# Attention blocks spread evenly over the token groups of queries, keys and values; W_o's first two weights split on GpSimd

## The chip, the cores and the metric

The kernel runs on one core of one Trainium2 chip. Its engines are TensorE (PE; PEld is its weight load), VectorE (DVE), ScalarE (ACT), GpSimd (POOL) and SyncE (SP, which here only issues loads and stores). The metric is the device time of one execution in microseconds. Of the kernel before there are three timed runs, 1322.33, 1322.56 and 1325.32 us; their median is 1322.56 us. A profile is taken of another execution.

## The reference, cut to what matters

Two decoder layers over 512 tokens of 1024 features in float32. The first mixes with a convolution module, the second with causal differential attention over 8 heads; each is followed by a SwiGLU FFN and by a gated per-layer input embedding. The change lies in the second layer's attention:

```python
def diff_attention(x, w_qkv, q_g, k_g, lq1, lk1, lq2, lk2, sub_g, w_o, rel_bias, lambda_init):
    qkv = x @ w_qkv
    q, k, v = jnp.split(qkv, 3, axis=-1)
    q = rms_norm(q.reshape(B, S, N_HEADS, 2, HEAD_DIM), q_g) * (HEAD_DIM ** -0.5)
    k = rms_norm(k.reshape(B, S, N_HEADS, 2, HEAD_DIM), k_g)
    v = v.reshape(B, S, N_HEADS, V_DIM)
...
        logits = jnp.einsum('bhcqd,bhckd->bhcqk', q_blk, k).astype(jnp.float32)
        logits = logits + bias[None, :, None]
        logits = jnp.where(dist >= 0, logits, -jnp.inf)
        probs = jax.nn.softmax(logits, axis=-1)
        w = probs[:, :, 0] - lam * probs[:, :, 1]
        return jnp.einsum('bhqk,bhkd->bhqd', w.astype(v.dtype), v)
...
    o = rms_norm(o, sub_g) * (1.0 - lambda_init)
    return o.reshape(B, S, N_HEADS * V_DIM) @ w_o
```

After it comes `h = h + swiglu(...)`, then `h = h + gate * (p[i] @ ple_w_proj[i])`. The product `p[i] @ ple_w_proj[i]` depends on no result of the layer, and the kernel computes it just behind the attention's slabs ("the projections" below).

## The kernel before, in words

**Products in three passes.** Every float32 product is computed with operands split into a high and a low part, as three matmuls (L142 to L144: low x high, high x low, high x high). A weight of 128x1024 is loaded by SP into a raw buffer (`wraw`, L133), ACT casts it to `whi` (L136), and DVE or POOL subtracts to get `wlo` (L137). There are 2 raw buffers and 4 each of `whi` and `wlo`. A load waits until the split of the weight that was in its raw buffer is done; a cast waits until PE is done with the weight that was in its `whi` buffer. The projections' input features pass through the same raw buffers (`pfeatures`, L238 load, L239 cast on ACT, L240 subtract on DVE).

**The slabs.** Queries with keys, and values, are computed in six slabs in the order of `QKV` (L69): q0, v0, q1, q2, v1, q3. A q slab holds queries and keys of a pair of heads, a v slab the values of four heads. A slab has four weights (`slab`, L556; from the second slab on its first weight is split on POOL, `GLO = 1`). It runs over four token groups of 128 tokens; each group is 24 matmuls of 512 columns into one PSUM tile (`tokens`, L564). A group of a q slab is a *unit*: ACT reads it twice (L600 scaled, L603 squared), DVE sums the squares (L607) and prepares them (L199), POOL raises to the power -1/2 (L201) and multiplies (L610), and then in `unit_end` PE transposes (L616), ACT writes queries and keys (L624, L625), POOL copies the keys' high part to the other half (L629), and DVE makes the remainders (L632, L634).

**The attention stages.** Every head has four blocks of 128 queries, and every block has three stages, 96 in all, in one list ordered so that a block's stages lie a few places apart: `stage_s` (PE scores L661, L662; DVE adds bias and takes the maximum L664; ACT exp L668; DVE combines L671 to L673), `stage_t` (PE transposes L681; ACT L683 and DVE L684 split), `stage_a` (PE with the values L697, L698; ACT L704, DVE L705; after a head's last block a norm, L709 to L719, POOL with L201 and L719). `stage_o` then transposes a finished head (L726) and splits it (`split_scaled`, L156 on ACT, L157 on DVE) into W_o's input. In the loop over the slabs the third item of a `QKV` entry gives for each token group how many steps of three stages are issued between its matmuls. The last `unit_end` follows the loop. What is left of the list is issued one stage at a time through `step()`: in the projections (L772 to L785, two weights, called P0 and P1 here, eight groups of six matmuls, L142 to L144 on `C` tiles), and then in W_o.

**W_o.** `linear` (L426) computes W_o's eight groups; the first two share a pass over the heads (`group0=2`), so their weights, called O0 and O1 here, are needed together. `first` says how many of these are split on POOL.

**What sets the order.** The program is handed to a scheduler that arranges each engine's instructions by its own model of their times; on the chip each engine then runs its list in order. An instruction that waits keeps all behind it on its engine waiting. PE's tiles come from 4 accumulators (`mm`), 2 score tiles (`sc`) and 2 transpose tiles (`tp`).

Of the kernel before, what the change touches and what calls it, by code (L numbers as in the profile page):

```python
# [23 lines left out]
NC = D // P  # L24
# [41 lines left out]
PACK = True  # L66
E1 = True
GLO = 1
QKV = (("q", 0, (0, 0, 0, 0)), ("v", 0, (0, 1, 1, 0)), ("q", 1, (1, 1, 2, 2)), ("q", 2, (0, 1, 2, 0)), ("v", 1, (1, 2, 2, 2)), ("q", 3, (0, 2, 0, 1)))  # L69


@with_exitstack
def trunk(ctx, tc, xT, pT, wts, diag, dww, vec, rel, onehot, lamv, out):
# [51 lines left out]
    def weight(n=1024, pieces=1, between=(), eng=V):  # L125
        i = wnext[0]
        wnext[0] += 1
        raw = sb([P, 1024], "wraw", 2)
        hi = sb([P, 1024], "whi", 4, F32R)
        lo = sb([P, 1024], "wlo", 4, F32R)  # L130
        for k in range(pieces):
            cut = slice(k * n // pieces, (k + 1) * n // pieces)
            nc.sync.dma_start(raw[:, cut], wts[i, :, cut])  # L133
            if k < len(between):
                between[k]()
            A.copy(hi[:, cut], raw[:, cut])  # L136
            eng.tensor_tensor(lo[:, cut], raw[:, cut], f(hi[:, cut]), ALU.subtract)  # L137
        return hi, lo

    def mm3(acc, a, b, first, last):  # L140
        (ah, al), (bh, bl) = a, b
        T.matmul(acc, al, bh, start=first, stop=False)  # L142
        T.matmul(acc, ah, bl, start=False, stop=False)  # L143
        return T.matmul(acc, ah, bh, start=False, stop=last)  # L144

    def wpart(w, k):
        return tuple(t[:, k * P : (k + 1) * P] for t in w)
# [254 lines left out]
    for m in range(NC):  # L402
        if m % 4 == 0:
            w = weight()
# [21 lines left out]
    def linear(n_in, src, consume, group0=1, before=None, after=None, first=0):  # L426


        m = 0
        while m < NC:  # L430
            g = group0 if m == 0 else 1
            ws = [weight(n_in * P, eng=G if m == 0 and i >= g - first else V) for i in range(g)]
            accs = [mm() for _ in range(g)]
            for k in range(n_in):
                if before:
                    before(k)
                for w_, a_ in zip(ws, accs):
                    mm3(a_, wpart(w_, k), src[k], k == 0, k == n_in - 1)
                    if after:
                        after()  # L440
            for i in range(g):
                consume(m + i, accs[i])
            m += g
# [112 lines left out]
    def slab(n=0):  # L556
        ws = [weight(eng=G if i < n else V) for i in range(4)]
        return [
            tuple(t[:, j * S : (j + 1) * S] for t in ws[k])
            for k in range(4)  # L560
            for j in range(2)
        ]
# [158 lines left out]
    ot = {}  # L721
# [22 lines left out]
    waiting = None  # L744
    for what, at, pace in QKV:
        ws = slab(GLO if at > 0 else 0)
# [27 lines left out]
    for m in range(NC):  # L774
        if m % 4 == 0:
            w = weight()
# [17 lines left out]
        V.tensor_tensor(h[m], acc, h[m], ALU.add)  # L794
        norm.chunk(m)

    linear(NC, ot, add_attn, 2, heads_until, step)
    n2 = Norm("ple_g1")
    ffn(norm, n2)

# [32 lines left out]
def _layout(a):  # L833
# [25 lines left out]
    qkv = a["attn_w_qkv"][0]  # L859
    for what, at, _ in QKV:  # L860
        if what == "v":
# [59 lines left out]
```

## Time and profile before

| | |
|---|---|
| median of three runs | 1322.56 us |
| the profiled execution | 1323.92 us |
| its span, first to last instruction | 1322.1 us |
| granted TensorE clock, mean | 0.986 of full |
| DMA | 91 GB/s mean |

The page gives for each engine the time in which it was busy. A row of a timeline has the start in us from the span's start, the duration, engine, line, operation, what is written and read with its shape, how many alike follow each other, and in brackets how long the engine stood idle before it and what it then waited for. Matmuls are pipelined: a row of 0.39 us is followed by the next 0.23 us later. A row of groups has the count, the total busy time, the mean of one in ns, and the idle time before with what ended it. A row of a table by stretches has the length and then each engine's busy time with its number of instructions, the granted clock, DMA's share and rate.

### The profile page before, as it was taken

The page shows a single profiled execution, that of the slowest core. Times are in us where ns is not written, and L with a number is a line of the kernel's source. Part 1 is how long each engine was busy: PE and PEld are TensorE (multiplying, and loading weights), DVE is VectorE, ACT ScalarE, POOL GpSimd, SP SyncE. Part 2 cuts the span into 40 slices and gives each one's busy share as a digit, 9 for nine tenths or more (in the row PEclk, how much of TensorE's full clock was granted, in tenths as well). Part 3 has the DMA queues.
Part 4 walks back from the last instruction along what each step waited for, and adds up shares of the span by engine and source line. Part 5 has one row for each costly group of instructions (what it writes and reads, how often), then busy time and mean ns, then how long its engine had stood idle before and what let it go on. Part 6 is the DMA issues. An engine that isn't in the chain of part 4 may idle for free. (4 is left out here: it accounts for less than half of the span.)

```text
span 1322.1 us, 15025 instructions
## 1 busy us (share of the span) xinstructions
PE 1284.4 (97%) x5686; PEld 1035.8 (78%) x5686; DVE 777.5 (59%) x1203; ACT 548.0 (41%) x862; POOL 303.8 (23%) x241
## 2 busy tenths in 40 slices
PE   8999879999999999999999998899999999999998
PEld 5766458888888888888888887778888888888887
DVE  6999984644344434455668897946543344334445
ACT  5676453422122212244466676734322222222342
POOL 5789852100000000022254544222000000000030
PEclk8999789999999999999999999999999999999999
DMA  6221112222222222222212221303222222222231
GB/s 222 90 104 52 51 32 86 90 96 96 100 96 99 100 100 96 80 101 101 91 64 81 103 73 36 108 34 126 97 96 96 96 98 100 103 94 93 78 121 64
DMA packets 37332, 120.40 MB, mean 91 GB/s; under 512 B 4323, under 2 KB 5475, under 8 KB 37260
## 3 DMA queue, kind: packets, MB, share of 16 engines
q1 hardware_dynamic: 35712, 117.06, 25.3%
q10 hardware_dynamic: 1548, 2.39, 0.6%
q8 instruction: 44, 0.72, 0.2%
q14 instruction: 28, 0.23, 0.0%
HBM read 117.31 MB, written 2.12 MB: 90 GB/s over the span
## 5 line engine op out<-in xcount | busy, mean ns | idle before, releaser
L136 ACT CAST whi<-wraw 128x1024 fp32r<-128x1024 f32 (+2 forms) x214 | 218.6, 1026 | 561.4 <-PE mm L144 351.3
L142 PE MATMUL mm<-A,wlo 128*128 128x512 f32 (+1 forms) x1096 | 426.8, 394 | 10.7 <-POOL C L597 6.0
L143 PE MATMUL mm<-A,whi 128*128 128x512 f32 (+1 forms) x1096 | 430.4, 394 | 0.2
L144 PE MATMUL mm<-A,whi 128*128 128x512 f32 (+1 forms) x1096 | 428.5, 391 | 0.0
L137 DVE TENSOR_TENSOR wlo<-wraw,whi 128x1024 fp32r<-128x1024 f32 (+2 forms) x207 | 259.1, 1255 | 62.4 <-ACT whi L136 62.3
L142 PEld LDWEIGHTS mm<-A,wlo 128*128 128x128 f32 x1096 | 208.2, 190 | 57.4 <-POOL C L597 6.8
L176 POOL TENSOR_TENSOR acc<-acc,wk 128x512 f32<-128x512 f32 x42 | 68.2, 1624 | 784.8 <-issue 671.2
L143 PEld LDWEIGHTS mm<-A,whi 128*128 128x128 f32 x1096 | 207.7, 190 | 47.4 <-DVE A L157 3.1
L144 PEld LDWEIGHTS mm<-A,whi 128*128 128x128 f32 x1096 | 207.8, 190 | 44.1 <-issue 1.9
L144 PE MATMUL mm<-B,whi 128*128 128x512 f32 x352 | 137.0, 389 | 0.0
L143 PE MATMUL mm<-B,whi 128*128 128x512 f32 x352 | 137.0, 389 | 0.0
L142 PE MATMUL mm<-B,wlo 128*128 128x512 f32 x352 | 136.4, 389 | 0.0
L305 POOL TENSOR_TENSOR wk<-wk,C 128x512 f32<-128x512 f32 x76 | 112.1, 1480 | 25.6 <-ACT C L304 19.6
L472 DVE TENSOR_TENSOR big<-mm,rb 128x512 f32<-128x512 f32 x44 | 30.4, 691 | 125.9 <-PE mm L144 125.9
L480 DVE TENSOR_TENSOR h<-mm,h 128x512 f32<-128x512 f32 x48 | 33.0, 691 | 120.9 <-PE mm L144 120.9
L470 DVE TENSOR_TENSOR big<-mm,rb 128x512 f32<-128x512 f32 x44 | 30.4, 691 | 99.3 <-PE mm L144 92.9
L143 PEld LDWEIGHTS mm<-B,whi 128*128 128x128 f32 x352 | 66.1, 188 | 13.7
L142 PEld LDWEIGHTS mm<-B,wlo 128*128 128x128 f32 x352 | 66.1, 188 | 13.7
L144 PEld LDWEIGHTS mm<-B,whi 128*128 128x128 f32 x352 | 66.1, 188 | 13.6
L144 PE MATMUL mm<-whi,A 128*128 128x512 f32 x192 | 75.7, 395 | 0.0
L143 PE MATMUL mm<-wlo,A 128*128 128x512 f32 x192 | 75.0, 396 | 0.0
L142 PE MATMUL mm<-whi,A 128*128 128x512 f32 x192 | 74.8, 397 | 0.0
(185 smaller groups left out, 1433.3 us busy)
## 6 DMA issues: line engine op xcount, KB each, us to landing
wraw<-in_wts SPq DMA_DIRECT2D x194, 512.0 KB, 3.4
wraw<-in_wts SPq DMA_DIRECT2D x16, 384.0 KB, 3.0
h<-in_xT SPq DMA_DIRECT2D x8, 256.0 KB, 5.7
bias<-scr ACTq DMA_DIRECT2D x8, 256.0 KB, 3.3
D<-in_diag SPq DMA_DIRECT2D x7, 256.0 KB, 3.9
out_t<-h SPq DMA_DIRECT2D x7, 256.0 KB, 2.0
wraw<-in_wts SPq DMA_DIRECT2D x4, 256.0 KB, 5.5
wraw<-in_pT SPq DMA_DIRECT2D x4, 256.0 KB, 2.9
```

The costliest lines, as they stand in the source:

```text
L136: A.copy(hi[:, cut], raw[:, cut])
L137: eng.tensor_tensor(lo[:, cut], raw[:, cut], f(hi[:, cut]), ALU.subtract)
L142: T.matmul(acc, al, bh, start=first, stop=False)
L143: T.matmul(acc, ah, bl, start=False, stop=False)
L144: return T.matmul(acc, ah, bh, start=False, stop=last)
L176: self.eng.tensor_tensor(self.acc, self.acc, sq, ALU.add)
L305: G.tensor_tensor(pacc, pacc, pr, ALU.add)
L470: V.tensor_tensor(tg, pg, rb, ALU.mult)
L472: V.tensor_tensor(tu, pu, rb, ALU.mult)
L480: V.tensor_tensor(h[m], acc, h[m], ALU.add)
```

## The change

```diff
-QKV = (("q", 0, (0, 0, 0, 0)), ("v", 0, (0, 1, 1, 0)), ("q", 1, (1, 1, 2, 2)), ("q", 2, (0, 1, 2, 0)), ("v", 1, (1, 2, 2, 2)), ("q", 3, (0, 2, 0, 1)))
+
+QKV = tuple((w, i, (n,) * 4) for w, i, n in (("q", 0, 0), ("v", 0, 1), ("q", 1, 1), ("q", 2, 1), ("v", 1, 2), ("q", 3, 1)))
...
-    linear(NC, ot, add_attn, 2, heads_until, step)
+    linear(NC, ot, add_attn, 2, heads_until, step, first=2)
```

The first edit gives every token group of a slab the same number of steps: none in q0, one in v0, q1, q2 and q3, two in v1. Before it was a number for each group. The second edit makes POOL, not DVE, split O0 and O1. The set of instructions is otherwise the same; the scheduler arranges all engines anew from the second slab to W_o. The changed file has one line more, so a line number behind L69 is one higher there.

## The prediction

> **What bounds the kernel now.** I read the page first, then the sums by stretches around the end of the query/key/value stage, then PE's timeline there.
>
> ```profile
> span 1322.1 us, 15025 instructions
> ...
> PE 1284.4 (97%) x5686; PEld 1035.8 (78%) x5686; DVE 777.5 (59%) x1203; ACT 548.0 (41%) x862; POOL 303.8 (23%) x241
> ```
>
> PE is busy for 97% of the span, so only what fills or opens a hole on PE can matter. The change touches one stage, and there the picture differs:
>
> ```profile
> core 0: us, PE busy (x) PEld busy (x) DVE busy (x) ACT busy (x) POOL busy (x), PEclk, DMA share, GB/s
> 653.50:818.00 164.50, 162.32 (x841) 137.22 (x841) 126.33 (x327) 106.56 (x240) 78.58 (x75) 1.00 0.22 73
> 818.00:830.80 12.80, 6.51 (x34) 5.20 (x32) 12.17 (x33) 9.76 (x23) 4.78 (x6) 0.79 0.30 102
> 830.80:844.30 13.50, 10.95 (x57) 8.22 (x56) 13.36 (x34) 11.08 (x26) 3.88 (x4) 0.95 0.46 158
> 844.30:884.20 39.90, 38.93 (x221) 33.58 (x219) 24.43 (x74) 19.98 (x48) 6.14 (x6) 1.00 0.08 27
> ```
>
> The first stretch is the six slabs of queries, keys and values: PE misses 2.2 us of 164.5. In the next two PE misses 8.8 us while DVE misses 0.8: the tail of the attention is bound by DVE and the chains through it. After 844.3 PE is full again.
>
> ```profile
> 817.64 0.39 PE L144 MATMUL mm<-whi,A 128*128 128x512 f32 x1
> ...
> 828.44 0.66 PE L661 MATMUL sc<-C,C 128*128 128x384 f32 x1 [2.55 <-DVE st L672]
> ...
> 829.22 1.05 PE L616 MATMUL tp<-ident,big 128*128 128x128 f32 x4
> ...
> 830.80 0.80 PE L142 MATMUL mm<-C,wlo 128*128 128x512 f32 x1
> ...
> 832.20 0.39 PE L142 MATMUL mm<-C,wlo 128*128 128x512 f32 x1
> 832.42 0.39 PE L143 MATMUL mm<-C,whi 128*128 128x512 f32 x1
> ...
> 841.27 0.47 PE L661 MATMUL sc<-C,C 128*128 128x512 f32 x1
> ...
> 844.29 0.39 PE L142 MATMUL mm<-C,wlo 128*128 128x512 f32 x1
> ...
> 856.58 0.39 PE L142 MATMUL mm<-A,wlo 128*128 128x512 f32 x1
> ...
> 884.21 1.19 PE L142 MATMUL mm<-A,wlo 128*128 128x512 f32 x4 [0.78 <-ACT A L156]
> ```
>
> I put a clock's zero at the end of the last slab matmul: 817.64 plus one spacing (832.20 to 832.42, so 0.23 per 512 columns), 817.87. Then the first projection matmul stands at +12.9, the last unit's transposes at +11.3, the last unit's scores (head 6, block 3) at +23.4, unbroken projections from +26.4, the first W_o matmul at +38.7, the last W_o block at +66.3.
>
> **The change, part by part.** The pace tuples add up to 21 steps before and 24 after, so 72 of 96 attention stages instead of 63 are issued inside the slabs, and 24 instead of 33 afterwards. No instruction is added; two wlo splits go from DVE to POOL. The rest is order, and the built program lists it for each engine. These rows price it:
>
> ```profile
> L137 DVE TENSOR_TENSOR wlo<-wraw,whi 128x1024 fp32r<-128x1024 f32 x6 | 8.1, 1347 | 0.3 <-ACT whi L136 0.3
> L136 ACT CAST whi<-wraw 128x1024 fp32r<-128x1024 f32 x6 | 6.3, 1049 | 3.7 <-DMA wraw<-in_wts 3.7
> L157 DVE SCALAR_TENSOR_TENSOR A<-tp,lam,A 128x512 fp32r<-128x512 f32 x8 | 5.9, 746 | 5.0 <-ACT A L156 4.9
> L719 POOL TENSOR_TENSOR D<-D,r 128x512 f32<-128x512 f32 x4 | 5.1, 1269 | 4.0 <-DVE r L717 2.9 <-ACT D L704 1.1
> L201 POOL TENSOR_TENSOR r<-v,mhalf 128x4 f32<-128x4 f32 x4 | 4.0, 1007 | 35.4 <-DVE v L199 35.3
> L634 DVE SCALAR_TENSOR_TENSOR C<-tp,vec,C 64x256 fp32r<-64x256 f32 x7 | 3.4, 484 | 0.1
> L629 POOL CAST C<-C 64x256 fp32r<-64x256 f32 x6 | 2.9, 488 | 10.4 <-ACT C L625 10.4
> L624 ACT ACTIVATE C<-tp,lam 64x256 fp32r<-64x256 f32 x5 | 2.3, 468 | 0.5 <-PE tp L616 0.4
> L664 DVE CUSTOM_DVE_ANT_0 big<-sc,bias 128x512 f32<-128x512 f32 x3 | 2.1, 684 | 0.0
> L600 ACT ACTIVATE big<-mm,rcol 128x512 f32<-128x512 f32 x1 | 0.7, 688 | 0.0
> L607 DVE TENSOR_REDUCE v<-wk 128x8 f32<-128x512 f32 x1 | 0.7, 686 | 0.0
> ...
> wraw<-in_wts SPq DMA_DIRECT2D x194, 512.0 KB, 3.4
> ```
>
> *Slabs.* Over the two built orders, matmul by matmul at 0.23 us per 512 columns, 2.7 us of PE work moves ahead of the zero: **+2.7** there, given back in the tail below. DVE has 23% of the stretch free; the even pace asks for six stages in each group of the second value slab, three in the other groups and none in the first slab, so nothing bunches as in the old q1 and q3, but DVE has nine more stages to do. New waits: 0 if the slack takes them, 3 if they double today's 2.2; I take **+1.0**, nearer to the slack.
>
> *Projection weights come sooner.* P0 and P1 (line 776) share the raw buffers with the feature loads, so P0's load waits for L240.
>
> ```profile
> 823.21 0.68 DVE L240 TENSOR_TENSOR C<-wraw,C 128x512 fp32r<-128x512 f32 x1
> ...
> 829.52 1.23 DVE L137 TENSOR_TENSOR wlo<-wraw,whi 128x1024 fp32r<-128x1024 f32 x1 [0.31 <-ACT whi L136]
> ...
> 837.02 1.97 DVE L137 TENSOR_TENSOR wlo<-wraw,whi 128x1024 fp32r<-128x1024 f32 x1
> ...
> 828.44 1.05 ACT L136 CAST whi<-wraw 128x1024 fp32r<-128x1024 f32 x1 [2.60 <-DMA wraw<-in_wts]
> ```
>
> L240 ends at 823.89, +6.0, today; the load starts and its cast, which waits for the landing, follows 4.5 us later; the split of 829.52 ends at 830.75 and the first projection matmul starts. In the new order L240 follows the evictions of q3's first unit, whose transposes stand 24 slab matmuls (5.5) and a few of the attention (0.7) ahead of the zero, at -6.2. Transposes 0.6, four ACT copies of 0.47, DVE's last remainders 0.7, L240 0.68: done at -2.3. Load 3.4 to 4.5, taken 3.9; cast 1.05; split 1.23: first projection matmul at **+3.9 instead of +12.9**.
>
> *W_o's splits.* O0 and O1, W_o's first two, are no hurry: the later of their old DVE splits, that of 837.02, ended 17.6 us ahead of 856.58. What counts is what they now stand before. ACT's new order puts O0's cast ahead of the last unit's read-out (L600, L603); POOL's puts O0's split ahead of that unit's L201 and O1's between L201 and L610. The old kernel did the same once:
>
> ```profile
> 749.49 1.63 POOL L201 TENSOR_TENSOR r<-v,mhalf 128x8 f32<-128x8 f32 x1 [2.94 <-DVE st L672]
> 751.09 2.40 POOL L137 TENSOR_TENSOR wlo<-wraw,whi 128x1024 fp32r<-128x1024 f32 x1
> 753.44 1.05 POOL L610 TENSOR_TENSOR big<-big,r 128x512 f32<-128x512 f32 x1
> ...
> 751.16 2.35 DVE L199 TENSOR_SCALAR v<-v 128x4 f32<-128x4 f32 x1 [0.29 <-POOL r L201]
> ```
>
> L610 came 2.4 us late. Walked: P0's split ends at +3.9, O0 lands at +7.5 (3.4 to 4.5 later), cast to 8.55, then L600 and L603 to 9.8 and L607 to 10.5. POOL: O0 8.6 to 11.0, a copy (0.49), L201 to 13.1, a copy. O1's load follows P1's DVE split (after P0's: four remainders, 1.9, a value remainder, 0.7, and 1.23, so +7.8) and lands by 11.5; its cast stands behind the third unit's four copies and three attention instructions and ends at 14.3; split to 16.7, L610 to 17.8, PE's transposes to 18.4 (+11.3 before, so 6 us later). Then four ACT copies, while POOL does L201 (1.0) and L719 (1.2) ahead of the L629 copy: last scores at +20.7. Everything behind them on PE waits, projections included. Next PE has five L726 groups on two tp buffers, each freed by an L157: DVE needs five L157 (3.7), two L664 of 512 (1.4), three small L664 (1.0), a 512 remainder (0.75) and small ones (1.0), and 0.5 of ACT waits: 8.3 us, so unbroken projections from **+29.0 instead of +26.4: +2.6**. Bounds: the old 3.0 us (26.4 less 23.4) gives 23.7, -2.7; O loads at 4.5 and each split followed by a wait give +33, +6.6.
>
> *The rest.* By the built orders 33.9 us of spaced PE work remain there against 34.8, which took 39.9: **-0.9**. PE has mostly stood idle since +6.7 by then. Today's restart ran slow: from 830.80 to 832.20 three matmuls took 1.40 instead of 0.69, with the granted clock at 0.79 over the idle stretch. Twelve projections restart: **+1.7**, between 0 and 2.8 (all twelve at half speed).
>
> Sum: 2.7 + 1.0 + 2.6 - 0.9 + 1.7 = **+7.1**, a span of 1329.2. The span lies in a run of 1323.92 us; the three timed runs have a median of 1322.56, so I add 7.1 to that: **1329.7**.
>
> The row of 751.16 shows more: a 128x4 DVE operation took 2.35 us while POOL split. [...]
>
> **The rivals.**
> - *Faster.* O0 and O1 land before ACT and POOL would otherwise reach them, so the early projections pay. Then L600 starts 2 us sooner, O1 costs L610 nothing (3.2), the last stretch takes the old 3.0 instead of 8.3, PE never cools: 7.1 - 2.0 - 3.2 - 5.3 - 1.7 = -5.1, 1317.5. For it: P0 comes 9 us sooner. Against: O0 can't be asked for before P0's split, +3.9; it decides from a landing before about +5.5. Chance 0.15.
> - *No change.* The walk holds up to the scores, but DVE, rid of two splits (2.5 us), then passes through as fast as today: 7.1 - 5.3 = +1.8, 1324.4. The holes only move. Chance 0.22.
> - *Slower still.* POOL's two splits each hold a DVE operation as long as 751.16's, in the tail where DVE is last: 2 x 2.35 = 4.7 more, 1334.4. For it: 13.36 busy of 13.5 us. Against: the walk's DVE waits for other things during half of the two splits. Chance 0.10.
> - *The slabs become DVE-bound*: waits of 6 instead of 1.0 there, +5: 1334.7. Against: DVE's free 23%. Chance 0.08.
>
> **How the numbers follow.** My forecast has 0.45. 0.3% is 4.0 us, about what a measurement of this kernel can tell. Faster by more than that: the first rival, 0.15. Within it: the second, 0.22, and 0.03 from the forecast's low edge, 0.25. Slower: what is left of the forecast and the last two, 0.60. The range is 1318 to 1338: it takes in the bounds of the load and of the clock, the second, third and fourth rivals, and leaves out half of the first and the far end of the walk's upper bound. The forecast's own range is 1326 to 1334.
>
> **What would show it.** Right: in the new timeline L240 ends before the last slab matmul; the first projection matmul comes 3 to 6 us after it; ACT has O0's cast with a wait for its load just ahead of L600; POOL has the second W_o split between L201 and L610; PE's last L616 is about 18 us after the zero, with a second idle stretch and a granted clock under 0.8. Wrong: a last L616 before +13, or DVE idle in the tail while PE waits; slab waits above 5 us would make it the fourth rival.

## The result, and the profile after

| | before | after |
|---|---|---|
| median, us | 1322.35 (5 runs, 1322.2 to 1325.32) | 1335.62 (5 runs, 1334.91 to 1338.07) |
| span of the profiled execution, us | 1322.1 | 1336.0 |

The ratio is 1.0099, with a 95% interval from 1.0088 to 1.0111: the change makes the kernel about 1% slower. The profiled execution of the changed kernel is the slowest of its five (1338.07 us); the span grew by 13.9 us, the median by 13.3. First the same stretches of the page as before: the six slabs, the tail up to where projections run unbroken, and from there to the last W_o block.

```profile
653.50:824.50 171.00, 165.99 (x859) 139.50 (x859) 131.08 (x347) 109.20 (x249) 75.60 (x74) 1.00 0.22 72
824.50:857.40 32.90, 19.30 (x90) 14.95 (x89) 26.88 (x65) 21.32 (x49) 14.44 (x14) 0.74 0.27 94
857.40:898.10 40.70, 38.31 (x200) 31.57 (x200) 17.67 (x53) 16.18 (x36) 4.09 (x4) 1.00 0.08 26
```

The second column is PE's busy time. In the slabs PE misses 5.0 us of 171.0 (before, 2.2 of 164.5). In the tail it misses 13.6 us of 32.9, at a granted clock of 0.74, and now DVE misses 6.0 there too: nothing is full. PE's timeline gives the points of the prediction's clock; its zero is 824.46 + 0.23 = 824.69.

```profile
824.46 0.39 PE L145 MATMUL mm<-whi,A 128*128 128x512 f32 x1
...
828.85 0.80 PE L143 MATMUL mm<-C,wlo 128*128 128x512 f32 x1 [2.05 <-DVE wlo L138]
...
833.54 0.60 PE L617 MATMUL tp<-ident,big 128*128 128x128 f32 x4
...
843.35 1.11 PE L617 MATMUL tp<-ident,big 128*128 128x128 f32 x4 [2.42 <-POOL big L611]
...
848.99 0.80 PE L662 MATMUL sc<-C,C 128*128 128x512 f32 x1 [3.67 <-POOL C L630]
...
857.48 0.39 PE L143 MATMUL mm<-C,wlo 128*128 128x512 f32 x1
...
898.02 1.20 PE L143 MATMUL mm<-A,wlo 128*128 128x512 f32 x4 [0.78 <-ACT A L157]
```

| step | before | forecast | after |
|---|---|---|---|
| zero, against before | | +3.7 | +6.8 |
| first projection matmul | +12.9 | +3.9 | +4.2 |
| last unit's transposes | +11.3 | +17.8 to 18.4 | +18.7 |
| last unit's scores | +23.4 | +20.7 | +24.3 |
| unbroken projections | +26.4 | +29.0 | +32.8 |
| last W_o block | +66.3 | | +73.3 |

So 6.8 us were lost in the slabs and 7.0 behind them. The list of PE's waits in the slabs, of before and then of after, shows what PE waited for (us in total, times, longest):

```profile
PE sc L661 <- DVE st L664: 1.6, 1, 1.6
PE mm L697 <- ACT wth L683: 0.6, 1, 0.6
```

```profile
PE sc L662 <- DVE st L665: 3.6, 4, 1.1
PE mm L698 <- ACT wth L684: 1.1, 1, 1.1
```

The waits of the slabs went from 2.2 to 4.7 us, in five holes; together with gaps too short for this list that makes PE's 5.0 us. In the tail, the timelines of POOL and DVE show what the two new splits did:

```profile
833.43 2.37 POOL L138 TENSOR_TENSOR wlo<-wraw,whi 128x1024 fp32r<-128x1024 f32 x1 [2.39 <-ACT whi L137]
...
839.94 2.35 POOL L138 TENSOR_TENSOR wlo<-wraw,whi 128x1024 fp32r<-128x1024 f32 x1
842.26 1.03 POOL L611 TENSOR_TENSOR big<-big,r 128x512 f32<-128x512 f32 x1
```

```profile
834.09 1.73 DVE L673 SCALAR_TENSOR_TENSOR st<-st,lam 128x1 f32<-128x1 f32 x1
840.59 1.72 DVE L673 SCALAR_TENSOR_TENSOR st<-st,lam 128x1 f32<-128x1 f32 x1
```

L611 followed O1's split at once, as walked, and one 128x1 operation of DVE, 0.22 us elsewhere, ended with each of the two splits (835.82 against 835.80, 842.31 against 842.29). All this made it tempting to read the tail as the price of the splits. The experiments say otherwise.

### The profile page after: what moved, and what is told of

Read it like the earlier page. It is cut to its first block, busy times and chain, and to the rows that moved or that the text cites. A ratio compares the mean times of both kernels' runs of the same rounds, so it can differ in the third digit from the quotient of the medians.

```text
span 1336.0 us, 15050 instructions
## 1 busy us (share of the span) xinstructions
PE 1289.2 (97%) x5686; PEld 1037.2 (78%) x5686; DVE 776.9 (58%) x1201; ACT 547.4 (41%) x862; POOL 304.7 (23%) x243
## 4 chain that ended last, share of the span: by engine, by line
PE 80%; POOL 6%; DVE 6%; ACT 2%; issue 2%; DMA 0%; POOLq 0%; ACTq 0%; DVEq 0%
PE mm L143 26%; PE mm L144 25%; PE mm L145 25%; POOL wk L306 5%; DVE sc L314 1%; PE mm L698 1%; PE sc L662 1%; DVE B L314 1%; POOL B L399 1%; DVE mm L314 1%; DVE wlo L138 1%; PE sc L663 1%; DVE C L635 1%; DVE C L633 0%; DVE st L673 0%
## 5 line engine op out<-in xcount | busy, mean ns | idle before, releaser
L143 PE MATMUL mm<-A,wlo 128*128 128x512 f32 (+1 forms) x1096 | 426.8, 393 | 10.7 <-POOL C L598 6.0
L138 DVE TENSOR_TENSOR wlo<-wraw,whi 128x1024 fp32r<-128x1024 f32 (+2 forms) x205 | 255.5, 1250 | 61.4 <-ACT whi L137 61.3
L143 PEld LDWEIGHTS mm<-A,wlo 128*128 128x128 f32 x1096 | 208.1, 190 | 57.4 <-POOL C L598 6.8
```

## The experiments

The profiled executions differ by up to 3.4 us ahead of the slabs, where the kernels are alike (the first slab matmul behind the bias table's product, L529, starts between 650.3 and 653.7 us), so stretches are compared: *slabs* from that matmul to zero, *tail* from zero to the last W_o block, and PE's idle time in the tail. All times are us; each ratio is to the kernel before on the same chip.

| kernel | slabs | tail | PE idle in it | median | ratio (95%) |
|---|---|---|---|---|---|
| before | 164.2 | 66.3 | 9.8 | 1322.35 to 1323.14 | |
| after | 171.1 | 73.3 | 16.0 | 1335.62 | 1.0088 to 1.0111 |
| e1_pace | 171.1 | 72.4 | 13.4 | 1334.75 | 1.0068 to 1.0098 |
| e2_wo | 164.2 | 66.4 | 10.5 | 1322.5 | 0.9991 to 1.001 |
| e3_one | 172.6 | 72.3 | 14.2 | 1335.54 | 1.0073 to 1.0106 |
| e4_behind | 171.1 | 73.3 | 17.7 | 1336.46 | 1.0083 to 1.0113 |
| f1_even21 | 169.0 | 66.4 | 7.8 | 1329.22 | 1.0029 to 1.0061 |
| f2_old24 | 172.2 | 68.2 | 11.7 | 1333.66 | 1.0066 to 1.0096 |
| f3_one_o | 171.0 | 74.3 | 17.2 | 1338.13 | 1.0104 to 1.0138 |
| f5_pfirst | 171.1 | 68.7 | 10.7 | 1329.24 | 1.004 to 1.007 |
| f6_before_pfirst | 164.2 | 65.1 | 8.4 | 1321.82 | 0.998 to 0.9998 |
| g2_pfirst_wk | 164.1 | 64.6 | 8.7 | 1320.34 | 0.997 to 0.999 |
| g1_border | 166.5 | 72.3 | 12.6 | 1330.47 | 1.0037 to 1.0068 |
| h1_late | 164.2 | 68.6 | 10.2 | 1324.58 | 1.0008 to 1.0026 |

The slabs of e3_one and f2_old24 are 1.5 and 1.1 us longer than those of the change although PE idles 5.0 us there in all three; the granted clock in them was 0.99 instead of 1.00.

**Each edit alone: e1_pace and e2_wo.** The first theory gave the slabs' 6.8 us to the pace and the tail's to the two splits.

```diff
# e1_pace, against after
-    linear(NC, ot, add_attn, 2, heads_until, step, first=2)
+    linear(NC, ot, add_attn, 2, heads_until, step)
# e2_wo, against before
-    linear(NC, ot, add_attn, 2, heads_until, step)
+    linear(NC, ot, add_attn, 2, heads_until, step, first=2)
```

> The even pace alone; both of W_o's first splits stay on DVE. Theory (two causes: the pace costs the slabs 6.8 us, the splits ahead of the last unit cost the tail 6.4): the slab stretch stays at 171 us with the last slab matmul at about 824.5; without 2.4 us splits in POOL's way the last unit's transposes come at +13 to +15 instead of +18.7 and unbroken projections from +26 to +29 instead of +32.8: span 1328 to 1332. Rival (the pace alone costs everything, also in the tail): 1334 to 1337. Rival (the splits alone): slabs back at 164 to 165, 1321 to 1325.

> The kernel before with W_o's first two splits on GpSimd alone; they stand behind the last unit's L610 on POOL in the built order. Theory: the slabs take 164.4 us as before; DVE is rid of 3.2 us of splits (1.23 and 1.97) in the tail, POOL's splits hold at most two DVE operations by 1.7 us: 1319 to 1324. Rival (the splits on POOL cost by themselves, wherever they stand): tail longer by 4 us or more, 1327 or more. Rival (pace alone costs): 1322, no difference.

The pace alone takes 1334.75 us: nearly all of the loss. Its slabs are those of the change, and its tail is 0.9 us shorter, not 6. PE's timeline of the pace alone (zero at 822.16) shows how that can be:

```profile
826.45 0.50 PE L143 MATMUL mm<-C,wlo 128*128 128x512 f32 x1 [2.17 <-DVE wlo L138]
...
829.68 0.60 PE L617 MATMUL tp<-ident,big 128*128 128x128 f32 x4
...
836.99 1.12 PE L617 MATMUL tp<-ident,big 128*128 128x128 f32 x4 [0.55 <-POOL big L611]
...
842.05 0.79 PE L662 MATMUL sc<-C,C 128*128 128x512 f32 x1 [3.10 <-DVE C L635]
...
851.96 0.63 PE L143 MATMUL mm<-C,wlo 128*128 128x512 f32 x1
852.40 0.63 PE L144 MATMUL mm<-C,whi 128*128 128x512 f32 x1
...
855.81 0.48 PE L143 MATMUL mm<-C,wlo 128*128 128x512 f32 x1
```

The last unit's transposes come at +14.8, inside the 13 to 15 that were expected without the splits. But unbroken projections come only at +29.8, 3.0 us sooner than in the change instead of 4 to 7, and run at half rate (0.43 us from one matmul to the next, 0.23 afterwards) for another 3.9 us, which takes 1.8 of the 3.0 back. And the early projections have a price of their own: PE waits 2.17 us for P0's weight with the third unit's transposes (829.68, +7.5) queued behind; before, those stood at +3.2. The splits alone, e2_wo, change nothing measurable: its interval holds 1.

**One split, and both behind the last unit: e3_one and e4_behind.** In the second, W_o's first two weights are issued only after the last unit's L611 (its `else` branch, as before, is left out here).

```diff
# e3_one, against after
-    linear(NC, ot, add_attn, 2, heads_until, step, first=2)
+    linear(NC, ot, add_attn, 2, heads_until, step, first=1)
# e4_behind, against after
-        G.tensor_tensor(q3, q3, rs.unsqueeze(2).to_broadcast([P, 8, DH]), ALU.mult)
+        last_unit[0] = G.tensor_tensor(q3, q3, rs.unsqueeze(2).to_broadcast([P, 8, DH]), ALU.mult)
...
+            if m == 0 and last_unit[0] is not None and first:
+                with tc.issue_after(last_unit[0].ins):
+                    ws = [weight(n_in * P, eng=G if m == 0 and i >= g - first else V) for i in range(g)]
```

> The change with O1's split alone on GpSimd (it still stands ahead of the last unit's L611); O0's is on DVE. Theory: slabs 171 us; O1 still costs L611 about 2.4 us and one DVE operation its 1.7 us, O0's hold of DVE is gone: last unit's transposes at +15 to +18, span 1331 to 1335, between the pace alone and the whole change. Rival (the pace costs all): as the change, 1336.

> The whole change, but W_o's first two weights are issued only behind the last unit's L611 on POOL. Theory (what costs is that the splits stand ahead of the last unit): last unit's transposes at +12 to +15, unbroken projections from +26 to +30, span 1328 to 1332, like the pace alone. Rival (what costs is that POOL's splits hold DVE, wherever they stand in the tail): the two holds of 1.7 us stay, unbroken projections from +30 or later, 1333 to 1336.

Neither differs from the change by what the intervals can tell. e4_behind is the telling one (zero at 824.02; its lines behind the edits stand five higher than those of the change). PE, POOL and DVE:

```profile
838.70 1.12 PE L622 MATMUL tp<-ident,big 128*128 128x128 f32 x4 [0.42 <-POOL big L616]
...
857.46 0.40 PE L143 MATMUL mm<-C,wlo 128*128 128x512 f32 x1
```

```profile
838.60 4.65 POOL L138 TENSOR_TENSOR wlo<-wraw,whi 128x1024 fp32r<-128x1024 f32 x2
```

```profile
838.62 2.35 DVE L678 SCALAR_TENSOR_TENSOR st<-st,lam 128x1 f32<-128x1 f32 x1
841.01 2.52 DVE L679 SCALAR_TENSOR_TENSOR big<-rb,st,big 128x256 f32<-128x256 f32 x1
```

The unit's transposes come at +14.7, 4 us sooner than in the change, and unbroken projections at +33.4, no sooner. Now the two splits fall on DVE from its first moment and hold it for 4.9 us, for work that takes under 0.9 (in the same profile L678 takes 0.22 at 845.84, and L679 0.62 at 846.09, for 128x384). In these kernels the place of the splits decides who waits, but hardly how long the tail is.

**Number or spread of the steps: f1_even21 and f2_old24.** The next theory was that the tail is set by the number of steps that the slabs take.

```diff
# f1_even21, against before: 2, 6, 3, 7, 3 steps as before, spread more evenly
+QKV = (("q", 0, (0, 0, 0, 0)), ("v", 0, (1, 0, 1, 0)), ("q", 1, (1, 2, 1, 2)), ("q", 2, (1, 1, 0, 1)), ("v", 1, (2, 2, 1, 2)), ("q", 3, (1, 1, 0, 1)))
# f2_old24, against before: three steps more
+QKV = (("q", 0, (0, 0, 0, 0)), ("v", 0, (0, 1, 1, 0)), ("q", 1, (1, 1, 2, 2)), ("q", 2, (0, 1, 2, 1)), ("v", 1, (2, 2, 2, 2)), ("q", 3, (0, 2, 1, 1)))
```

> The kernel before with the same number of steps in each slab (21 in all), only spread more evenly inside each slab; W_o as before. Theory (the number of steps costs, not their spread: 24 steps leave behind the slabs nothing but the chain of the last heads): last W_o block at +66 to +67 after the last slab matmul as before, slabs 164 to 166 us, time 1321 to 1325. Rival (the even spread itself makes the waits in the slabs and the long tail): slabs 168 or more, tail +70 or more, 1329 or more.

> The kernel before with its uneven pace and three steps more, in q2, v1 and q3 (24 in all, as in the change); W_o as before. Theory (the number of steps costs): last W_o block at +72 to +73 after the last slab matmul as in the pace alone; slabs 167 (2.7 of work more) to 169 us: 1330 to 1334. Rival (the even spread costs): tail and waits as before, 2.7 of work only moved: 1321 to 1324.

Half right each. With 21 steps the tail is that of before, 66.4, whatever their spread. But the spread alone costs the slabs 4.8 us without one stage more (PE's waits in them, f1_even21):

```profile
PE tp L681 <- DVE C L634: 3.0, 3, 1.5
PE sc L661 <- DVE st L664: 1.3, 2, 0.9
PE mm L143 <- DVE wlo L137: 1.2, 1, 1.2
```

(Its five runs lie between 1325.45 and 1330.24, and the profiled one is the fastest, so the 4.8 may be more in others.) With 24 steps in the old, uneven manner the slabs take 172.2 and the tail only 1.8 more than before, not 6: in the profiled execution number alone does not explain the tail. (That execution is again the fastest, 1331.14 us of up to 1334.26. Both profiles start their slabs early, at 650.3 and 650.8, which can account for most of these spreads, but the slower executions have no profile.)

**The order of PE in the tail: f3_one_o and f5_pfirst.** PE's built order showed a tie. Accumulators are handed out in the program's order, and in the built orders no projection group stands ahead of the first product into the accumulator handed out before its own. In the change the third group's predecessor belongs to head 6's first product with the values; before, three groups came ahead of that product. So in the change PE has two projection groups, and then no other projection until +32.8. f5_pfirst issues four groups ahead of that. f3_one_o tests another suspicion, that the five L727 due at once hold the transpose tiles.

```diff
# f3_one_o, against after
-        while done[0] < NH and (n - LA - 3) // 4 > done[0]:
+        if done[0] < NH and (n - LA - 3) // 4 > done[0]:
# f5_pfirst, against after
-        step()
+        if m >= 4:
+            step()
...
-        pp.append(project(ph, m, w, o, step))
+        pp.append(project(ph, m, w, o, step if m >= 4 else (lambda: None)))
```

> The whole change, but at most one finished head is transposed (L727) after each stage instead of all that are due at once; the same work in another order. Theory (the five L727 in a row on two tp buffers and five L158 on DVE hold head 6's first transposes, its first product with the values and, behind that in the order of the accumulators, all later projections): the third projection group comes at +26 to +30 instead of +32.8, the tail is 2 to 4 us shorter, 1331.5 to 1334. Rival (the tail is bound by DVE's and ACT's chain of the last units, whatever stands where on PE): 1335 to 1337.

> The whole change, but no stage is issued during the first four projection groups, so that four instead of two of them stand ahead of head 6's products on PE; the stages follow during the last four groups and W_o. Theory (PE idles in the tail because projections that depend on no attention are held behind head 6 in program order): PE does 2.8 us more work in the holes between +4 and +20, the granted clock stays higher, tail 2.5 to 5 us shorter: 1330.5 to 1333. Rival (the chain of the last units sets the tail and the stages then simply come later): 1335 to 1338.

f3_one_o is no faster: its third group does come sooner (851.55, +28.1), but the time behind it grows by more, and the tail is 0.9 us longer. f5_pfirst is 6.4 us faster than the change. Its two stretches of the tail:

```profile
823.00:857.20 34.20, 24.90 (x116) 20.19 (x115) 23.42 (x65) 24.85 (x56) 15.58 (x14) 0.85 0.34 106
857.20:891.70 34.50, 33.17 (x173) 27.79 (x172) 17.14 (x50) 13.14 (x30) 4.10 (x4) 0.96 0.05 16
```

Against the change's 13.6 us, PE idles 9.3 in the first, and its clock is 0.85 instead of 0.74; the tail is 68.7. The slabs, and with them the slab waits, are those of the change, and the last unit's transposes stand where they did (841.89, +18.9). So a late last unit does not by itself make the tail this long: with the unit as late, 4.6 of the 7.0 us come back once PE has other work in the meantime. Two things limit this. The same edit also shortens the tail of the kernel before, by 1.3 us (f6_before_pfirst below), so some 3.3 of the 4.6 belong to the change. And the number of groups ahead of head 6 is not the whole account, as f2_old24 shows. It too has 24 steps and only two groups ahead, and yet a tail of 68.2 (zero at 822.95):

```profile
825.15 0.50 PE L142 MATMUL mm<-C,wlo 128*128 128x512 f32 x1 [0.23 <-DVE wlo L137]
...
850.42 0.39 PE L142 MATMUL mm<-C,wlo 128*128 128x512 f32 x1
```

Its first projection stands at +2.2 where e1_pace has +4.3, its unbroken projections at +27.5 instead of +29.8, and they run at 0.23 us from one matmul to the next at once.

**The border of slabs: g1_border.** Of the change's five holes in the slabs one lies at a border, where v1 begins; the others are inside v0 and v1. DVE's timeline of the change there, and PE's:

```profile
754.15 1.22 DVE L138 TENSOR_TENSOR wlo<-wraw,whi 128x1024 fp32r<-128x1024 f32 x1
...
760.70 0.42 DVE L665 CUSTOM_DVE_ANT_0 big<-sc,bias 128x256 f32<-128x256 f32 x1
```

```profile
761.19 0.38 PE L662 MATMUL sc<-C,C 128*128 128x256 f32 x1 [1.00 <-DVE st L665]
```

DVE works without a gap from the split of the next slab's weight to the L665 that frees the score tile. The old pace had no step in the last group of q2 and one in the first of v1; the new one has one and two.

```diff
# g1_border, against after
+QKV = (("q", 0, (0,) * 4), ("v", 0, (1,) * 4), ("q", 1, (1,) * 4), ("q", 2, (1, 1, 1, 0)), ("v", 1, (1, 2, 2, 2)), ("q", 3, (1,) * 4))
```

> The whole change, but the last group of q2 takes no step and the first of v1 one instead of two (22 steps in all). Theory (waits in the slabs come where steps meet the splits of the next slab's weights on DVE at a border of slabs): of the 6.8 us of holes in the slabs the 1.8 between 756 and 762 go, the others stay; slabs 171.1 less 1.8 less 1.8 of work moved behind: 167 to 168. Rival (the extra steps overload the stage as a whole and the waits turn up elsewhere): holes 6 to 8 us, slabs 169 to 170. The tail is expected between that of 21 and of 24 steps, 505 to 511 from the last slab matmul to the end.

```profile
PE sc L662 <- DVE st L665: 1.2, 2, 1.0
PE mm L698 <- ACT wth L684: 0.6, 1, 0.6
```

PE's waits in the slabs fall from 4.7 to 1.8 us, more than expected, since two of the later holes went too. The slabs take 166.5: 4.6 us less, of which 3.0 is idle time of PE (5.0 to 2.0, less than before the change) and 1.6 is less busy time, mostly work moved behind. The edit shows that these two steps bring the waits; that it is their meeting with the split is read from the one timeline, and was not tested by moving the split. The tail stays at 72.3 with 22 steps and two projection groups ahead of head 6.

**The same lever without the change: f6_before_pfirst, g2_pfirst_wk, h1_late.** The first two put four projection groups first in the kernel before; the second also loads the features into another buffer, so that P0's load need not wait for them. h1_late does the reverse.

```diff
# f6_before_pfirst, against before: the edit of f5_pfirst
# g2_pfirst_wk, against f6_before_pfirst
-            raw = sb([P, 1024], "wraw", 2)[:, :S]
+            raw = sb([P, 1024], "wraw", 2)[:, :S] if layer == 0 else wk()
# h1_late, against before
     pp = []
+    for _ in range(3):
+        step()
```

> The kernel before (its pace, W_o on DVE) with no stage issued during the first four projection groups. Theory (in the tail PE lacks work because projections are held behind the attention, in the kernel before too: 9.8 us of holes behind the last slab matmul): tail 1 to 4 us shorter, 1318 to 1321.5. Rival (before, DVE sets the tail with 25.7 busy of 26.4 us, so stages issued later only come later): 1322 to 1325.

> As the kernel before without stages in the first four projection groups, and the projections' features are loaded into a work buffer instead of the raw weight buffers, so that the load of their weights need not wait for L240. Theory (the first projections can fill the holes between +4 and +13 where PE waits for the last units): first projection at +4 to +9 instead of +12.9, tail 2 to 6 us shorter than before, 1316 to 1320. Rival (filling these holes only leaves the later ones empty, as in the change, where the first projection stood at +4.2): 1321 to 1326.

> The kernel before with its pace (21 steps in the slabs), but three steps are issued ahead of the first projection, so that 24 of the 32 steps stand before it, as in the change, and the third projection group stands behind head 6's first product instead of ahead of it. Theory (what makes the tail long is how many projection groups PE may do before head 6's products): slabs 164.2 us as before, tail from the last slab matmul to the end 508 to 511 instead of 504.2, 1326 to 1330. Rival (what counts is how many steps were done inside the slabs): tail 504 to 505, 1321.5 to 1324.

f6_before_pfirst shortens the tail by 1.3 us, about as little as a measurement can tell. g2_pfirst_wk is the best kernel of the study, 1320.34 us, 0.1 to 0.3% below before. Its tail:

```profile
815.68:843.90 28.22, 21.55 (x115) 16.29 (x114) 26.36 (x67) 22.82 (x53) 10.01 (x10) 1.00 0.33 102
843.90:880.28 36.38, 34.35 (x195) 28.92 (x194) 21.73 (x71) 16.77 (x43) 6.14 (x6) 1.00 0.05 15
```

The first projection stands at +5.4, hardly later than in the change; more groups follow between the attention's pieces, and PE's clock stays at 1.00. The tail is 1.8 us shorter than before, just short of the 2 to 6 that were expected. As f6_before_pfirst already gains 1.3, the earlier weight adds only 0.5.

The expectation of h1_late miscounts: three calls are three stages, one step of the pace, so 22 of 32 steps stood ahead of the projections; the place of the third group is as stated. That group comes at 843.87, +27.8 instead of +16.6, and the tail is 68.6:

```profile
816.08:843.88 27.80, 18.41 (x87) 14.89 (x86) 26.63 (x70) 21.24 (x49) 8.80 (x10) 0.75 0.39 124
843.88:884.72 40.84, 40.05 (x224) 34.15 (x222) 23.10 (x69) 19.82 (x47) 6.50 (x6) 1.00 0.08 26
```

That is 2.3 us for holding one group back, most of it clock (0.75, and PE busy 58.5 for the same work as 56.5 before), between what the two theories said. With the old pace 2.7 us more of the attention's work lies behind the zero and may give PE work in the meantime; this was not tested.

## Why the prediction was right, and where it was not

Direction and range held (1329.7 forecast, 1318 to 1338; 1335.62 measured). But the size was nearly double, and the forecast's own range, 1326 to 1334, was missed. The third and fourth rivals, with 1334.4 and 1334.7, came nearer, but the runs show neither's mechanism as the cause. So the wide range held, not the sum: its three parts measure 6.8 instead of 3.7 up to the zero, 6.4 instead of 2.6 from there to unbroken projections, and 0.6 instead of 0.8 behind them.

*Slabs.* The "+1.0" of new waits was mis-sized. The zero moved by 6.8; with the 2.7 of moved work from the built orders as forecast, the rest is 4.1, not 1.0: 2.8 are more idle time of PE (5.0 instead of 2.2), and in the other 1.3 PE is busy for longer at a granted clock of 1.00. f1_even21 shows as much (163.4 us against 162.0) with no stage added, but no run here explains it. The step that failed is its reason, DVE's free 23% of the stretch. The waits are local: g1_border removes 2.9 us of them by taking one step from each side of one border, and f1_even21 makes waits with no stage added. An average of free time says nothing on a border where DVE also splits the next slab's weights. The fourth rival, a DVE-bound stage, is not what happened: DVE is busy 131 of 171 us.

*Projection weights come sooner.* Right: +4.2 for +3.9, with a half-rate restart from 828.85 to 832.00 (0.43 us from one matmul to the next, at a granted clock of 0.50), and O0's cast and both POOL splits in the order of the walk, the second 0.9 us later.

*W_o's splits.* The dates came out (transposes of the last unit +18.7 for 17.8 to 18.4, which is 7 us later than before and not the 6 of the walk), the cause did not. "Everything behind them on PE waits" is true, but without the splits (e1_pace) the unit is 3.8 us earlier and the tail 0.9 us shorter; with the unit early and the splits behind it (e4_behind) nothing is gained; with the unit late and PE supplied (f5_pfirst) 4.6 of the tail's 7.0 us come back. What the walk missed is what PE could do meanwhile. The term "+2.6" measured 6.4. The step from scores to unbroken projections, 8.3 forecast, took 8.5, but the scores themselves were 3.6 later than forecast. The step of the walk that failed is the one from the last unit's transposes to its scores, 2.3 us for four ACT copies and one POOL copy; it took 5.6:

```profile
845.40 0.61 ACT L669 ACTIVATE acc<-acc,st 128x384 f32<-128x384 f32 x1 [3.99 <-DVE st L665]
```

```profile
847.44 1.04 POOL L720 TENSOR_TENSOR D<-D,r 128x512 f32<-128x512 f32 x1 [1.51 <-DVE r L718]
```

ACT's copies stood behind an exp, and POOL's copy behind L720, and both of these waited for DVE. The walk had also left out the two holds of DVE, 1.5 us each (1.73 against 0.22), ahead of these; but they are the smaller part, since the pace alone, with both splits on DVE, takes 5.1 us for the same step (+14.8 to +19.9). One sign of being wrong came in part: DVE idles 6.0 us in this tail, 2.2 of them while PE idles too (before, 0.8 and 0.2).

*The third rival*, POOL's splits that hold DVE, exists with almost the price given to it (1.7 us each in the change, 2.35 and 2.52 in e4_behind), but the tail is not DVE-bound after the change, so the end moves by less than 1 us; and on DVE the splits cost 1.2 us each themselves. e2_wo shows the balance: zero.

*The clock.* The tail's 7.0 us can be written as 6.2 more idle, less 2.7 of work moved out, and the rest, 3.5, is PE busy for longer with the same work: 57.4 against 56.5 less 2.7. That is twice the 1.7 taken for the restart, and it came elsewhere. The 1.7 was meant for the twelve projections that begin the unbroken ones; in the change these ran at a granted clock of 1.00 from 857.48 on, and the half rate came earlier, behind 828.85 and behind 848.99 (granted clock 0.50 from 828.85 to 832.00 and from 848.99 to 852.00). That the last stretch still grew by about what was forecast is luck: PE idles 2.4 us in it instead of 1.0. The half rate itself is in the rows: 0.43 from matmul to matmul from 851.96 to 855.81 in e1_pace, a stretch of 3.9 us, and 0.23 afterwards. What sets the length of such a stretch no run shows.

*What stays open.* The tail of the pace alone is 6.0 us longer than before's. Holding one group back costs 2.3 with the old pace (h1_late). f2_old24, with 24 steps and the same two groups ahead, costs 1.8, so the two do not add up. Of the 4.2 that remain between f2_old24 and the pace alone, 2.3 come before the unbroken projections and 1.9 behind them, where only the pace alone runs at half rate. Why the even pace makes the first projection 2.1 us later there, and how much of the rest comes from the granted clock (0.78 before the unbroken projections and 0.95 behind them in the pace alone, 0.81 and 1.00 in f2_old24), was not separated.

## What to carry to other kernels

When stages are moved ahead out of a chain-bound tail, the chain does not get shorter; look for what PE has left to do beside it, and in which order buffers are handed out, before counting the moved work as won. A pace that looks irregular may be fitted to the borders where another load falls on the same engine, and an engine's average slack does not price a step there. A date that comes out as walked does not prove its cause: only the version without it does.

## What the runs showed of the hardware that was not expected

That a split on POOL can hold a DVE operation was in the profile before; new is that it did so in each of three places where the splits were put, and that it mattered so little. While POOL split a 128x1024 weight (2.35 to 2.4 us), DVE operations as small as 128x1 lasted until the split's end: 1.73 and 1.72 us in the change, 2.35 and 2.52 in e4_behind, and in e2_wo:

```profile
833.57 2.37 POOL L137 TENSOR_TENSOR wlo<-wraw,whi 128x1024 fp32r<-128x1024 f32 x1 [1.30 <-ACT whi L136]
```

```profile
833.91 2.05 DVE L717 TENSOR_TENSOR r<-r,r 128x4 f32<-128x4 f32 x1
```

Each of them reads two tensors; the operation of 751.16, held for 2.35 us (a 128x8 one of the same line took 0.17 at 749.17), reads one. Which operations of DVE are held no run separates. Moving a split of 1.2 us from DVE to POOL therefore freed little of DVE here, as long as DVE had an operation due that was held.
